# Merged strided loads of stacked operands, and earlier loads, in a two-layer encoder kernel

## The chip, the cores and the metric

The kernel runs on one core of one Trainium2 chip. The metric is the device time of one execution in microseconds (us). Three runs of the kernel before gave a median of 2371.69 us (2371.62 to 2374.82).

## What is computed

Two layers of a bidirectional encoder work on a sequence of 512 tokens, 1024 channels wide, in float32. Each layer is a half-step feed-forward network, a mixer with three kinds of attention, and a second half-step feed-forward network, every one between two RMS norms:

```python
for l in range(DEPTH):
    y = swiglu(rmsnorm(h, ffn1_pre_g[l]), ffn1_w_gu[l], ffn1_w_down[l])
    h = h + 0.5 * rmsnorm(y, ffn1_post_g[l])
    u = rmsnorm(h, mix_pre_g[l])
    proj = u @ w_in[l]
    qa, ka, va, qb, kb, vb, qc, kc, vc, gl = jnp.split(proj, split_at, axis=-1)
    oa = neighbourhood_attention(qa, ka, va, na_rpb[l])     # A: 8 heads of 64, with a bias table
    ob = sliding_window_attention(rope(qb), rope(kb), vb, sw_sink[l])    # B: 8 heads, 2 of k and v
    oc = differential_attention(rope(qc), rope(kc), vc, lam, ...)  # C: 4 heads, two softmax maps each
    gates = sigmoid(gl + b_gate[l])
    merged = sum over the branches of gate * (branch @ w_branch[l])
    h = h + rmsnorm(merged @ w_out[l], mix_post_g[l])
    y = swiglu(rmsnorm(h, ffn2_pre_g[l]), ffn2_w_gu[l], ffn2_w_down[l])
    h = h + 0.5 * rmsnorm(y, ffn2_post_g[l])
```

## The kernel before

**Precision.** Matmuls run on float32r operands. Each float32 operand is split in a high part (ScalarE copies it) and a low part (VectorE subtracts), and a product is two or three matmuls of such parts. For attention scores, where a head is only 64 channels deep, the two parts are stacked on the 128 partitions: a stack holds 64 rows of the high part above 64 rows of the low part. For keys there is a second stack with low above high. The score of a block is then two matmuls, with the query's stack against both stacks of the key (`softmax_pv`, L1675).

**Stages.** A layer passes through three pools of on-chip buffers: the feed-forward network ("f"), the projection ("p", `project`) and the mixer ("m", `mixer`). `project` computes u @ w_in for all blocks of 128 channels that the attention needs (QA, KA, VA, QB, KB, VB, QC, KC, VC, four or one of each), and keeps most of the results in DRAM: the high and low parts of a block as two tensors of 128 x 512 ("part", L1427), and the blocks of QC and KC as they are ("raw", L1474), since their rotary turn is done later. All these stores go through `store` (L1403) on GpSimd's DMA queue.

**The mixer's order.** `ORDER` is a list written out by hand of the units of work: `qa`, `qb` and `qc` load what one attention pair or head needs, `aa`, `ab` and `ac` are the attention itself, `ga`, `gb`, `gc` the gates, `ya`, `yb`, `yc` the products with w_branch. `do` traces one unit. A planner then orders each engine's instructions from this trace and its own estimate of times; that order is fixed in the program, on the engines and on the DMA queues alike. An engine that waits holds up everything behind it.

**The loads.** All loads of the mixer but those of weights go through SyncE's queue (SP). `restacked` (L1774) loads a stack in two halves of 64 partitions, one from the high tensor and one from the low (L1783, L1784): 30 stacks a layer, into 14 buffers "st". `rope` (L1762) loads a raw block (L1760), and a second time with the two halves of each map exchanged, in four loads of 32 partitions (L1768); it then multiplies by the cosine and sine tables (L1769, L1770) and adds (L1771). These blocks live in five buffers "tx". The tables are loaded at unit `kb` (`tables_in`, L1943). `ask` (L1729) loads the raw relative-position values of a head of A, at the unit `qa` of its own pair and behind its stacks; its DRAM side is a hand-made pattern of 8 x 16 rows of 2 KB. `biases` (L1732) builds from it an edge tile and a middle tile for the head, in buffers "g".

**What stands behind what.** In `softmax_pv`, VectorE makes the low part (L353) of the transposed weights, which TensorE multiplies at L1710. The weights of the dense products are split by L224 (ScalarE) and L225 (VectorE) and multiplied at L326 to L328.

Of the kernel before, what the change touches and what calls it, by code (L numbers as in the profile page):

```python
# [10 lines left out]
F32 = mybir.dt.float32  # L11
# [5 lines left out]
P = 128  # L17
# [3 lines left out]
T = 512  # L21
# [18 lines left out]
QA, KA, VA, QB, KB, VB, QC, KC, VC, GL = 0, 4, 8, 12, 16, 17, 18, 22, 26, 30  # L40
# [79 lines left out]
def encoder_kernel(ctx: ExitStack, tc: tile.TileContext, order, xT, wts, cols, rows, rpb, consts, tables, out):  # L120
    nc = tc.nc
# [5 lines left out]
    dr = ctx.enter_context(tc.tile_pool(name="dr", bufs=1, space=bass.MemoryType.DRAM))  # L127
# [19 lines left out]
    def nm(s):  # L147
        serial[0] += 1
        return f"{s}{serial[0]}"

    def big(tag, dt=F32, shape=(P, T), name="v"):
        if tag in BUFS:
            return sb.tile(list(shape), dt, tag=tag, name=nm(name), bufs=BUFS[tag])
        kind, pool = phase[0]
        return pool.tile(list(shape), dt, tag=tag, name=nm(name), bufs=ABUFS[kind][tag])
# [7 lines left out]
    V, A, G, PE = nc.vector, nc.scalar, nc.gpsimd, nc.tensor  # L163

    def f(t):
        return t.bitcast(F32)
# [94 lines left out]
    for l in range(L):  # L261
        for which in (1, 2):
            name = f"ffn{which}_w_down"
# [1104 lines left out]
    def project(l, op, accs):  # L1368
# [34 lines left out]
        def store(kind, x):  # L1403
            d = dr.tile([P, T], F32, tag=kind, name=nm(kind), bufs=60)
            G.dma_start(d, f(x))
            return d

        def parts(x):
            hi, lo = big("t", F32R, name="hi"), big("t", F32R, name="lo")
            A.activation(hi, x, AF.Copy)  # L1410
            V.tensor_tensor(out=lo, in0=x, in1=f(hi), op=ALU.subtract)
            return hi, lo

        def stacked(c, x):
            hi, lo = parts(x)
            if c in (QA, KA):
                made[c] = []
                for s in range(2):
                    own, res = slice(64 * s, 64 * s + 64), []
                    for one, two in ((hi, lo), (lo, hi))[: 1 if c == QA else 2]:  # L1420
                        st = slots.pop(0)
                        nc.sync.dma_start(f(st)[0:64], f(one)[own])
                        nc.sync.dma_start(f(st)[64:128], f(two)[own])
                        res.append(st)
                    made[c].append((res + [None])[:2])
                return
            made[c] = store("part", hi), store("part", lo)  # L1427

        def turned(c, x, heads):
            tp = bank("at")  # L1430
# [13 lines left out]
        turning, slowly, values = [], [], []  # L1444
# [19 lines left out]
        def ready(c, x):  # L1464
            if c >= GL:
                gated(c, x)
            elif c < VA:
                stacked(c, x)
            elif QB <= c < VB:
                turned_by(c, x)  # L1470
            elif c < KB or c >= VB and (c < QC or c >= VC):
                values.append(lambda: turned(c, x, 1 if c >= VC else 2))
            else:
                made[c] = store("raw", x)  # L1474

        def now():
            while values:
# [8 lines left out]
        made = {}  # L1486
# [38 lines left out]
        for n, c0 in (("cosR", 0), ("sinR", 512)):  # L1525
            t = big("rr", name=n)
# [108 lines left out]
        work(len(slowly))  # L1635
        return made

    def raw_of(l, hd):
        return bass.AP(rpb.tensor, (l * 8 + hd) * 16 * RPBW, [[RPBW, 8], [1, 16], [1, 8 * RPBW]])

# [76 lines left out]
    def mixer(l, op, made):  # L1717
# [3 lines left out]
        for n in range(3):  # L1721
            masks[n] = pre[:, n // 2, 256 * (n % 2) : 256 * (n % 2) + 256]

        def ask(hd):
            if hd < 2:
                raws[hd] = pre[:, 2 + hd, :]
                return
            raw = raws[hd] = big("g", name="braw")
            nc.sync.dma_start(raw, raw_of(l, hd))  # L1729

        def biases(hd):
            raw = raws.pop(hd)  # L1732
            if hd < 2:
                edge = made["edges"][:, hd, :]
                mid = made["edges"][:, 2, 2 * P * hd : 2 * P * (hd + 1)]
            else:
                edge = big("g", name="bedge")
                mid = big("g", shape=(P, 2 * P), name="bmid")

            def put(dst, mask, n0, n1):  # L1740

                src = raw[:, 7 * RPBW + 39 - 8 * n0 :]
                (ps0, pn), _ = src.ap
                V.tensor_tensor(
                    out=dst.rearrange("p (d r c) -> p d r c", r=8, c=8),
                    in0=bass.AP(src.tensor, src.offset, [[ps0, pn], [-8, n1 - n0], [-RPBW, 8], [-1, 8]]),
                    in1=mask.rearrange("p (d r c) -> p d r c", r=8, c=8),
                    op=ALU.add,
                )

            put(edge[:, 0:256], masks[0], 0, 4)
            put(mid, masks[1], 0, 4)
            put(edge[:, 256:384], masks[2][:, :P], 2, 4)
            put(edge[:, 384:512], masks[2][:, P:], 0, 2)
            return lambda i: edge[:, 0:256] if i == 0 else edge[:, 256:512] if i == NT - 1 else mid


        def load(d, dt=F32, tag="tx"):
            x = big(tag, dt, name="x")
            nc.sync.dma_start(f(x), d)  # L1760
            return x

        def rope(c):
            x = load(made[c])
            sh = big("tx", name="sh")
            for q in range(4):
                o = q ^ 1
                nc.sync.dma_start(sh[32 * q : 32 * q + 32], made[c][32 * o : 32 * o + 32])  # L1768
            V.tensor_tensor(out=x, in0=x, in1=turning[0], op=ALU.mult)  # L1769
            V.tensor_tensor(out=sh, in0=sh, in1=turning[1], op=ALU.mult)  # L1770
            V.tensor_tensor(out=x, in0=x, in1=sh, op=ALU.add)  # L1771
            return x

        def restacked(c, both):  # L1774
            if c in (QA, KA):
                return made[c]
            hi, lo = made[c]
            res = []
            for s in range(2):
                own, pair_ = slice(64 * s, 64 * s + 64), []  # L1780
                for one, two in ((hi, lo), (lo, hi))[: 2 if both else 1]:
                    st = big("st", F32R, name="st")
                    nc.sync.dma_start(f(st)[0:64], one[own])  # L1783
                    nc.sync.dma_start(f(st)[64:128], two[own])  # L1784
                    pair_.append(st)
                res.append((pair_ + [None])[:2])
            return res

        def values(c):
            t = made[c] if c == VA else [load(d, F32R, "st") for d in made[c]]  # L1790
            if c >= VC:
                return t
            v = [x.rearrange("p (b h d) -> p b h d", b=2, h=2) for x in t]
            return lambda j, s: v[j // 2][:, j % 2, s, :]
# [4 lines left out]
        def settle():  # L1799
            while pending:  # L1800
                pending.pop(0)()
# [4 lines left out]


        def qkv_a(p):
            got = restacked(QA + p, False), restacked(KA + p, True), values(VA + p)
            for s in range(2):  # L1810
                ask(2 * p + s)
            return got

        oa = [sb.tile([P, 4, T], F32R, tag="X", name=nm("oa"), bufs=BUFS["X"]) for _ in range(2)]

# [121 lines left out]
        def qkv_b(c):  # L1937
            return restacked(c, c == KB)

        def tables_in():  # L1940
            for n, c0 in (("cosR", 0), ("sinR", 512)):
                t = big("rr", name=n)
                nc.sync.dma_start(t, tables[:, c0 : c0 + T])  # L1943
                turning.append(t)
# [22 lines left out]
        def do(u):  # L1967
            kind, i = u[:2], int(u[2:] or 0)
            if kind == "fc" or kind[0] == "y":
                if kind == "fc" and i >= len(oc) or kind[0] == "y" and (kind[1], 3) not in OT:  # L1970
                    settle()
            if kind == "qa":
                held[u] = qkv_a(i)
            elif kind == "kb":
                tables_in()
                held["kb"] = qkv_b(KB), values(VB)
            elif kind == "qb":
                held[u] = qkv_b(QB + i)
            elif kind == "qc":
                held[u] = qkv_c(i)  # L1980
            elif kind == "aa":
                attn_a(i, *held.pop(f"qa{i}"))
            elif kind == "ab":
                attn_b(i, held.pop(f"qb{i}"), *held["kb"])
            elif kind == "ac":
                attn_c(*held.pop(f"qc{i}"))
            elif kind == "fc":
                finish_c(i)
            elif kind[0] == "g":
                gates("abc".index(kind[1]), i)  # L1990
            elif kind[0] == "y":
                combine("abc".index(kind[1]), kind[1], i)
# [15 lines left out]
        at = len(order) // HB  # L2008
# [56 lines left out]
        first = begin(H.X.blocks, firsts_of(l, 2), ("mm", "mx"), ((1, second_block), (KD - 2, last_block)))  # L2065
# [5 lines left out]
    for l in range(L):  # L2071
        with open_phase("f"):
            X, accs = ffn(l, 1, X, accs)
        with open_phase("p"):
            made = project(l, X, accs)
# [63 lines left out]
```

## Time and profile before

| | |
|---|---|
| median of three runs | 2371.69 us (2371.62 to 2374.82) |
| the profiled execution | 2370.88 us |
| its span, first to last instruction | 2369.1 us |
| mean granted TensorE clock | 0.996 |
| TensorE / VectorE / ScalarE / GpSimd busy | 99% / 80% / 61% / 9% |
| DMA | 395.16 MB, mean 167 GB/s |

The profile comes from one execution under the hardware profiler. PE is TensorE's matmuls, PEld its weight loads, DVE VectorE, ACT ScalarE, POOL GpSimd, SP SyncE; a "q" behind the name is the engine's sequencer, which waits and issues DMAs. `L1769` is a line of the kernel. `x<-raw` means that an instruction writes tile x and reads tensor raw. In lists of waits the columns are the total, the number and the longest, in us; in a timeline the start, the duration and in brackets the idle time before, with what ended it. A table of stretches gives the start and end, the length, the busy time of PE, PEld, DVE, ACT and POOL with instructions in brackets, the granted clock of TensorE as a share, the mean busy share of the 16 DMA engines (over 1 where packets overlap) and GB/s. A row of one line's instructions gives the shortest, median and longest duration in ns and the first and last start in us. DMA queue q1 is that of SP, q10 that of ScalarE, q0 that of GpSimd; a row of a queue gives packets, MB and busy share of the 16 engines, a row of issues the count, the size and the median us from issue to landing.

### The profile page before, as it was taken

To read this page: it belongs to the slowest core of one execution; us is meant where nothing else is said; L and a number is where in the kernel's file an instruction comes from. 1 tells how busy PE (TensorE), PEld (TensorE's weight loads), DVE (VectorE), ACT (ScalarE), POOL (GpSimd) and SP (SyncE) were. 2 spreads that over 40 slices of the span, in tenths; PEclk is the share of its full clock that TensorE was granted. 3 is DMA by queue.
4 is the path that set the end of the run, shared out by engine and by line. 5 is a ranking of instruction groups with operands and counts; after the bars stand their busy time and mean duration, and the time that the engine had idled before them with its cause. 6 is when DMAs were issued, how large, how long until landed. Compare 5 with 4: busy or idle time off the path is not lost. (4 is left out here: it accounts for less than half of the span.)

```text
span 2369.1 us, 40269 instructions
## 1 busy us (share of the span) xinstructions
PE 2342.6 (99%) x15134; PEld 2109.5 (89%) x15134; DVE 1892.4 (80%) x3082; ACT 1446.8 (61%) x2715; POOL 223.8 (9%) x354
## 2 busy tenths in 40 slices
PE   9999999999999999999999999999999999999998
PEld 8999889997888889998899998889978788899987
DVE  7887988966888668888878878889579876788796
ACT  6555566667777465655655554666687764556563
POOL 0111001110121001110001110011101200011100
PEclk9999999999999999999999999999999999999999
DMA  5566446667565524664525565276774664256642
GB/s 170 162 169 190 154 145 187 207 219 207 168 174 189 167 97 147 166 162 165 175 87 168 162 178 196 102 216 199 222 206 139 195 206 140 97 147 172 190 148 84
DMA packets 138147, 395.16 MB, mean 167 GB/s; under 512 B 19296, under 2 KB 26080, under 8 KB 137440
## 3 DMA queue, kind: packets, MB, share of 16 engines
q1 hardware_dynamic: 102960, 260.37, 35.0%
q0 software_dynamic: 20160, 78.66, 12.4%
q10 hardware_dynamic: 14832, 53.56, 7.4%
q8 instruction: 119, 1.95, 0.3%
q14 instruction: 76, 0.62, 0.1%
HBM read 326.98 MB, written 80.74 MB: 172 GB/s over the span
## 5 line engine op out<-in xcount | busy, mean ns | idle before, releaser
L680 PE MATMUL mm<-X,h 128*128 128x256 f32 x1504 | 268.0, 278 | 1.2 <-DVE v L738 1.2
L680 PEld LDWEIGHTS mm<-X,h 128*128 128x128 f32 x1504 | 228.5, 188 | 2.5 <-DVE v L738 2.0
L225 DVE TENSOR_TENSOR w<-wr,w 128x512 fp32r<-128x512 f32 x264 | 178.9, 685 | 56.2 <-ACT w L224 55.2
L224 ACT ACTIVATE w<-wr 128x512 fp32r<-128x512 f32 x264 | 162.5, 627 | 96.4 <-PE mm L328 40.8
L326 PE MATMUL mm<-X,w 128*128 128x512 f32 (+1 forms) x570 | 218.3, 383 | 1.8 <-ACT X L553 1.8
L328 PE MATMUL mm<-X,w 128*128 128x512 f32 (+1 forms) x570 | 216.4, 380 | 0.8 <-DVE w L225 0.8
L327 PE MATMUL mm<-X,w 128*128 128x512 f32 (+1 forms) x570 | 216.2, 379 | 0.8 <-DVE X L554 0.7
L680 PE MATMUL mm<-ht,h 128*128 128x256 f32 x752 | 210.1, 279 | 0.0
L680 PE MATMUL mm<-ht,l 128*128 128x256 f32 x752 | 210.1, 279 | 0.0
L680 PE MATMUL mm<-lt,h 128*128 128x256 f32 x752 | 209.4, 278 | 0.0
L680 PE MATMUL mx<-ht,h 128*128 128x256 f32 x752 | 208.3, 277 | 0.6 <-ACT v L724 0.6
L680 PE MATMUL mm<-X,l 128*128 128x256 f32 x752 | 208.2, 277 | 0.0
L680 PE MATMUL mx<-ht,l 128*128 128x256 f32 x752 | 208.1, 277 | 0.0
L680 PE MATMUL mx<-lt,h 128*128 128x256 f32 x752 | 207.9, 277 | 0.0
L630 DVE TENSOR_TENSOR l<-wr,h 128x1024 fp32r<-128x1024 f32 x94 | 114.9, 1222 | 65.7 <-PE mm L680 65.7
L662 ACT ACTIVATE h<-wr 128x1024 fp32r<-128x1024 f32 x94 | 99.9, 1062 | 78.7 <-PE mx L680 55.5
L680 PE MATMUL at<-X,w 128*128 128x256 f32 x1128 | 144.2, 277 | 0.0
L680 PEld LDWEIGHTS mx<-ht,h 128*128 128x128 f32 x752 | 141.2, 188 | 1.4 <-ACT v L724 1.4
L680 PEld LDWEIGHTS mm<-ht,l 128*128 128x128 f32 x752 | 141.7, 188 | 0.1
L680 PEld LDWEIGHTS mm<-ht,h 128*128 128x128 f32 x752 | 141.7, 188 | 0.0
L680 PEld LDWEIGHTS mm<-lt,h 128*128 128x128 f32 x752 | 141.7, 188 | 0.0
L680 PEld LDWEIGHTS mx<-ht,l 128*128 128x128 f32 x752 | 141.2, 188 | 0.2 <-DVE l L640 0.2
(458 smaller groups left out, 6802.4 us busy)
## 6 DMA issues: line engine op xcount, KB each, us to landing
wr<-in_wts_dram SPq DMA_DIRECT2D x273, 512.0 KB, 4.6
wr<-in_wts_dram ACTq DMA_DIRECT2D x102, 512.0 KB, 4.1
sum<-in_wts_dram POOLq DMA_DIRECT2D x64, 512.0 KB, 5.3
st<-part SPq DMA_DIRECT2D x120, 128.0 KB, 5.1
ap<-in_wts_dram SPq DMA_DIRECT2D x20, 512.0 KB, 5.6
a<-kept SPq DMA_DIRECT2D x32, 256.0 KB, 6.3
ap<-sum SPq DMA_DIRECT2D x16, 512.0 KB, 4.3
x<-part SPq DMA_DIRECT2D x32, 256.0 KB, 3.8
```

The source lines that it names most:

```text
L224: A.activation(hi, raw, AF.Copy)
L225: V.tensor_tensor(out=lo, in0=raw, in1=f(hi), op=ALU.subtract)
L326: PE.matmul(acc, w[0], x[0], start=start, stop=False)
L327: PE.matmul(acc, w[0], x[1], start=False, stop=False)
L328: PE.matmul(acc, w[1], x[0], start=False, stop=stop)
L630: V.tensor_tensor(out=w["l1"], in0=self.raws[g][0], in1=f(w["h1"]), op=ALU.subtract)
L662: A.activation(self.W[g]["h24"], self.raws[g][1], AF.Copy)
L680: PE.matmul(acc, ws[i], xs[j], start=start and k == m == 0, stop=stop and k == n - 1 and m == 2, skip_group_check=True,)
```

## The change

Four things change, all between the projection and the mixer's attention:

- **Stacks by one strided transfer.** The parts of a block are stored in one DRAM tensor, high rows, then low rows, and for keys the high rows a third time. A stack is then one load of 128 partitions, whose DRAM side is a pattern made by `halves`: two runs of 64 rows, 128 rows apart.
- **Raw blocks twice.** A QC or KC block is stored twice, in rows interleaved so that the block and the block with exchanged halves are each one load by `halves`, at row 0 and at row 32.
- **Biases a pair ahead.** The raw values of heads 2 and 3 are asked for with the first pair, ahead of the stacks, and so on; the middle tiles of two heads share one buffer.
- **Tables and first raw blocks.** The rotary tables and the two loads each of the first QC and the first KC block are issued at unit `qa1` instead of at `kb` and `qc0`.

```diff
@@ project: stacked, ready
-            made[c] = store("part", hi), store("part", lo)
+            n = 2 + (KA <= c < VA or c == KB)
+            d = dr.tile([n * P, T], F32, tag=f"both{n}", name=nm("both"), bufs=60)
+            for at, t in enumerate((hi, lo, hi)[:n]):
+                G.dma_start(d[P * at : P * at + P], f(t))
+            made[c] = d
...
-                made[c] = store("raw", x)
+                made[c] = dr.tile([2 * P, T], F32, tag="raw", name=nm("raw"), bufs=60)
+                for n in range(2):
+                    G.dma_start(halves(made[c], 64 * n), f(x))
...
+    def halves(d, row):
+        pitch = d.ap[0][0]
+        return bass.AP(d.tensor, d.offset + row * pitch, [[P * pitch, 2], [pitch, 64], [1, T]])
@@ mixer: biases, rope, restacked, qkv_a, do
+        mids = []
...
-                mid = big("g", shape=(P, 2 * P), name="bmid")
+                if hd % 2 == 0:
+                    mids.append(big("g", name="bmid"))
+                mid = mids[-1][:, 2 * P * (hd % 2) : 2 * P * (hd % 2) + 2 * P]
...
+        def begun(c):
+            x = load(halves(made[c], 0))
+            sh = big("tx", name="sh")
+            nc.sync.dma_start(sh, halves(made[c], 32))
+            return x, sh
+
+        first = {}
+
         def rope(c):
-            x = load(made[c])
-            sh = big("tx", name="sh")
-            for q in range(4):
-                o = q ^ 1
-                nc.sync.dma_start(sh[32 * q : 32 * q + 32], made[c][32 * o : 32 * o + 32])
+            x, sh = first.pop(c, None) or begun(c)
...
-            hi, lo = made[c]
             res = []
             for s in range(2):
-                own, pair_ = slice(64 * s, 64 * s + 64), []
-                for one, two in ((hi, lo), (lo, hi))[: 2 if both else 1]:
+                pair_ = []
+                for n in range(2 if both else 1):
                     st = big("st", F32R, name="st")
-                    nc.sync.dma_start(f(st)[0:64], one[own])
-                    nc.sync.dma_start(f(st)[64:128], two[own])
+                    nc.sync.dma_start(f(st), halves(made[c], P * n + 64 * s))
                     pair_.append(st)
...
         def qkv_a(p):
-            got = restacked(QA + p, False), restacked(KA + p, True), values(VA + p)
-            for s in range(2):
-                ask(2 * p + s)
-            return got
+            for hd in ((0, 1, 2, 3), (4, 5), (6, 7), ())[p]:
+                ask(hd)
+            return restacked(QA + p, False), restacked(KA + p, True), values(VA + p)
...
             if kind == "qa":
+                if i == 1:
+                    tables_in()
+                    first.update((c, begun(c)) for c in (QC, KC))
                 held[u] = qkv_a(i)
             elif kind == "kb":
-                tables_in()
                 held["kb"] = qkv_b(KB), values(VB)
```

## The prediction

> **What bounds the kernel now.** I read the page first, then the busy time by stage, the waits of PE, the timelines around the longest wait, and the DMA view of that stage.
>
> ```profile
> span 2369.1 us, 40269 instructions
> PE 2342.6 (99%) x15134; PEld 2109.5 (89%) x15134; DVE 1892.4 (80%) x3082; ACT 1446.8 (61%) x2715; POOL 223.8 (9%) x354
> ```
>
> PE is busy 2342.6 of 2369.1 us. Nothing that shortens a load can win more than the 26.5 us in which PE is idle. The profiled execution took 2370.88 us, 1.8 us around its span and 0.03% under the median of 2371.69; the sum below is made against 2371.
>
> The change touches the mixer. These are its attention stretches in layers 0 and 1 (columns: PE, PEld, DVE, ACT, POOL busy, granted clock, DMA share, GB/s):
>
> ```profile
> 514.00:720.00 206.00, 201.53 (x1070) 169.16 (x1068) 160.78 (x457) 153.31 (x389) 30.01 (x56) 0.98 0.67 190
> 1690.00:1900.00 210.00, 204.75 (x1078) 171.04 (x1077) 164.93 (x465) 156.32 (x393) 30.59 (x58) 0.99 0.67 184
> ```
>
> About 5 us idle in each, and a clock a little below full. The waits of PE name one place, and the timelines of PE and DVE show it in both layers:
>
> ```profile
> PE o L1710 <- DVE lo L353: 6.9, 2, 3.7
> ...
> PE o L1892 <- DVE lo L353: 1.2, 1, 1.2
> ...
> 557.87 0.58 PE L1710 MATMUL o<-lo,x 128*128 128x256 f32 x1 [3.67 <-DVE lo L353]
> ...
> 556.73 0.69 DVE L1769 TENSOR_TENSOR x<-x,cosR 128x512 f32<-128x512 f32 x1 [5.60 <-DMA x<-raw]
> 557.34 0.17 DVE L1692 RECIPROCAL l<-l 128x4 f32<-128x4 f32 x1
> 557.43 0.39 DVE L353 TENSOR_TENSOR lo<-at,hi 128x256 fp32r<-128x256 f32 x1
> ...
> 1729.85 0.39 PE L1710 MATMUL o<-lo,x 128*128 128x256 f32 x1 [3.21 <-DVE lo L353]
> ...
> 1728.70 0.69 DVE L1769 TENSOR_TENSOR x<-x,cosR 128x512 f32<-128x512 f32 x1 [5.13 <-DMA x<-raw]
> ```
>
> DVE stands 5.60 us at the first rotary multiply, whose block has not landed, and the low half that PE needs is queued behind it. The clock is then halved for a while:
>
> ```profile
> 556.50:563.33 6.83, 5.46 (x14) 4.45 (x15) 3.00 (x9) 3.34 (x8) 0.00 (x0) 0.50 0.93 218
> 1730.69:1734.10 3.41, 3.41 (x9) 2.67 (x9) 1.58 (x5) 2.17 (x6) 0.00 (x0) 0.50 0.98 217
> ```
>
> **Part 1: tables, first raw blocks and biases earlier.** The tables and the four loads of the first two rotary blocks move from behind the third pair's stacks to ahead of the second pair's. If they land, 3.67 + 3.21 us of waiting go, and half of 6.83 + 3.41 us at half clock: 6.9 + 5.1 = **12.0 us**. Next late in the mixer is, by the same view, the 1.2 us at L1892. The shared middle bias tile saves buffers and no instruction; the rpb loads go a pair earlier. Both cost nothing on PE, since no row of PE waits for a bias. But on SP's queue everything moved now stands ahead of the second pair's stacks, which part 3 needs.
>
> **Part 2: more stores.** Each layer gets four third copies (KA+1 to KA+3, KB) and eight second raw stores, 24 more on POOL in all:
>
> ```profile
> L1405 POOL DMA_DIRECT2D raw<-v x8: 542/542/542, 459.2 to 1673.6; - x8
> ...
> L1729 SPq DMA_DIRECT2D braw<-in_rpb_dram x12: 622/643/665, 526.5 to 1733.4; - x12
> ...
> L1784 SPq DMA_DIRECT2D st<-part x60: 444/594/1198, 495.8 to 1770.0; - x60
> ```
>
> 24 x 0.54 = 13 us of POOL, which is busy 9%, and nobody waits soon for these stores: nothing. SP issues 60 stack loads where it issued 120, and 16 rotated loads where it issued 64. Even if one strided issue costs what a bias load costs (643 ns, also a hand-made pattern), SP gains; it sets no end, so nothing.
>
> **Part 3: the shape of the merged loads.** This decides. A merged load reads DRAM as 2 runs of 64 rows: its outermost dimension is 2. Before, all loads have 32, 64 or 128 rows outermost, but one: the bias load reads 8 x 16 rows. The DMA view of 514 to 720 us lets one count what an outermost 8 does:
>
> ```profile
> DMA packets 16984, 39.13 MB, mean 190 GB/s; under 512 B 3118, under 2 KB 3118, under 8 KB 16965
> ...
> q1 hardware_dynamic: 10592, 17.83, 32.1%
> ...
> st<-part SPq DMA_DIRECT2D x58, 128.0 KB, 4.9
> x<-part SPq DMA_DIRECT2D x14, 256.0 KB, 4.6
> ...
> x<-raw SPq DMA_DIRECT2D x8, 256.0 KB, 3.6
> sh<-raw SPq DMA_DIRECT2D x32, 64.0 KB, 2.0
> ...
> braw<-in_rpb_dram SPq DMA_DIRECT2D x6, 256.0 KB
> ...
> cosR<-in_tables_dram SPq DMA_DIRECT2D x1, 256.0 KB, 7.4
> sinR<-in_tables_dram SPq DMA_DIRECT2D x1, 256.0 KB
> x<-gate SPq DMA_DIRECT2D x1, 256.0 KB
> ```
>
> Every row here is 2 KB, so SP's 121 loads are 58 x 64 + 14 x 128 + 8 x 128 + 32 x 32 + 6 x 128 + 3 x 128 = 8704 row packets. Queue q1 has 10592; 1888 are left, tiny ones. If each load ended with one on each of 16 engines there would be 121 x 16 = 1936. The 48 missing are 6 x 8: 115 loads ended on 16 engines and the six bias loads on 8. So the outermost dimension caps the engines, and I read the merged loads as running on **2 engines of 16**, 64 rows (131 KB) each.
>
> By the Trainium skill, "DMA: Bandwidth & Descriptors", section "Why a DMA increments its semaphore by 16 and not by 1", a DMA runs on the largest number up to 16 that divides the slowest dimension of both patterns, and from SP on the lowest-numbered engines. The count above agrees with the first half at 8; no run here shows 2. That rule speaks against the change, and by it the sum is the one that follows.
>
> Which two? No view numbers the engines. The first x<-raw was issued behind two bias loads:
>
> ```profile
> 544.95 1.81 SPq L1729 DMA_DIRECT2D braw<-in_rpb_dram  x2
> ...
> 548.06 0.43 SPq L1760 DMA_DIRECT2D x<-raw  x1
> ```
>
> It landed by 556.73, some 8.7 us after issue, where the median of its kind is 3.6. If bias loads took their engines in turn, two of them would have spread like one weight load. I take it that it is always the same engines, and so that all merged loads share one pair.
>
> The rate of one engine comes from three rows: the whole engine set in its fullest microsecond of this stage, in one of its fullest stretches anywhere, and q1 in the stack stretch, 516 to 640 us:
>
> ```profile
> 553.00:554.00 1.00, 1.00 (x6) 0.59 (x4) 0.00 (x0) 0.30 (x2) 0.00 (x0) 1.00 1.04 361
> ...
> 766.00:768.00 2.00, 2.00 (x16) 1.83 (x16) 1.97 (x4) 1.09 (x3) 0.00 (x0) 1.00 1.04 417
> ...
> DMA packets 11170, 24.25 MB, mean 196 GB/s; under 512 B 1886, under 2 KB 1886, under 8 KB 11159
> ...
> q1 hardware_dynamic: 8179, 13.88, 42.1%
> ...
> x<-raw SPq DMA_DIRECT2D x3, 256.0 KB, 3.6
> sh<-raw SPq DMA_DIRECT2D x12, 64.0 KB, 2.3
> ```
>
> 361 / (16 x 1.04) = 21.7 GB/s, so 6.0 us a load; 417 / 16 = 26.1, so 5.0 us; 13.88 MB / (0.421 x 16 x 124 us) = 16.6, so 7.9 us under full contention. I take 6.0: while the stage is stretched, the other traffic thins out, but it does not go.
>
> When are the loads wanted?
>
> ```profile
> 516.27 0.44 SPq L1783 DMA_DIRECT2D st<-part  x1
> ...
> L1675 PE MATMUL mx<-st,st x112: 274/282/442, 531.2 to 646.8; 128*128 128x256 f32 x80, 128*128 128x384 f32 x32
> ...
> L1769 DVE TENSOR_TENSOR x<-x,cosR x8: 675/681/692, 556.7 to 718.8; 128x512 f32<-128x512 f32 x8
> ```
>
> - *516 to 640 us*, before the last head of the stacks: 30 stack loads (60 of L1784 in two layers) and the four early raw loads, 34 x 6.0 = 204 us on each of the two engines. Their share of the rest: 24.25 MB less the 9.2 MB of stack, raw and rotated loads in that stretch (58 x 128 KB, 3 x 256 KB, 12 x 64 KB), over 16, is 0.94 MB, 43 us. 247 us of work for 124: **123 us late**. Fourteen stack buffers let SP run ahead by under two pairs, so the lateness cannot be hidden by starting sooner; and the first score matmul on stacks, 15 us after the loads begin, waits at once.
> - *640 to 720 us*, the rotary blocks of heads 1 to 3: 12 loads, 72 us. The rest: 39.13 - 24.25 = 14.9 MB less 2.6 of raw and rotated loads, over 16, 0.77 MB, 36 us. 108 us for 80: **28 us late**.
>
> PE's order is fixed, and no work of PE stands behind to fill in, so lateness is PE idle. 151 us a layer, 302 in two, less the 12.0 of part 1: 2371 + 302 - 12 = **2661 us**. At 5.0 us a load: (170 + 36 - 124) + (60 + 29 - 80) = 91 a layer, 2541. At 7.9: (269 + 57 - 124) + (95 + 46 - 80) = 263 a layer, 2885. The half clock after each wait adds nothing while the loads are what is late; where they are not, it takes the time up.
>
> **The rivals.**
> - *Sixteen engines after all* (the pattern is cut up again before it reaches the engines, so part 3 does not happen): 2371 - 12 = 2359 us, faster. For it: the stall is real and the loads for it now start some 30 us sooner. The Trainium skill's same page, "Rules for kernel authors", says that two transfers to halves of the partitions should rather be one over 128, which is this outcome; no row here shows such a pair merged. Against it: the six bias loads were not cut up again. The point that decides is the wire time of a merged load: under 124 / (34 + 43 / 6.0) = 3.0 us nothing is late in the stack stretch, and over it lateness there grows by some 41 us a layer for each us. Chance 0.09.
> - *Two engines, taken in turn*: no engine is overfull, each load only lands some 3 us later (5.0 to 7.9 us of wire where 4.9 was the median landing). Stacks are asked for 15 us or more ahead and stand it; the rotary chain of heads 1 to 3, four loads a head, may give 12 us a head and all of the gain back: from 2359 to 2359 + 72, about 2385. Against it: the 8.7 us above. Chance 0.07.
> - *The wait only moves*: the early loads land, but stand ahead of the second pair's stacks on SP, and PE waits there for what it saved: 2371. For it: 15 us between 516.27 and 531.2. Chance 0.04.
>
> **How the numbers follow.** The overfull pair of engines has 0.80 and is the forecast, 2661. Its own range is 2541 to 2885; the unknown clock and a start of some loads before 516 us widen it, and a part of the in-turn case lies near its foot: 2490 to 2940 should hold the time 8 times in 10. About 0.2% is what a measurement of this kernel can tell from no change. Slower: 0.80 and most of the in-turn case, 0.86. Faster: nearly all of the sixteen-engine case, 0.09. Same: 0.05, from the moved wait.
>
> **What the changed profile would show.** Right: q1's tiny packets fall to 2 for each merged load; st and x landings in tens of us; PE waiting for st loads in the mixer for 100 us or more a layer, the granted clock often 0.50 there, the other stages unchanged. Part 1 right: no 5.6 us wait at L1769's first multiply. Wrong: st loads landing in 5 us with DMA share near 0.67, or a mixer of some 206 us.

## The result, and the profile after

| | before | after |
|---|---|---|
| median of five runs | 2371.62 us (2366.04 to 2374.82) | 2757.03 us (2754.78 to 2762.81) |
| ratio, 95% interval | | 1.1638 (1.1614 to 1.1662) |
| the profiled execution, its span | 2370.88, 2369.1 us | 2762.81, 2761.0 us |
| mean granted clock | 0.996 | 0.931 |

The kernel became 385 us slower. The forecast was 2661 us, with a range of 2490 to 2940 and a chance of 0.86 for slower: side and range held, and 96 us more were lost than forecast.

The page after begins with these two lines:

```profile
span 2761.0 us, 40158 instructions
PE 2412.5 (87%) x15134; PEld 2159.3 (78%) x15134; DVE 1901.4 (69%) x3082; ACT 1447.3 (52%) x2715; POOL 244.3 (9%) x378
```

TensorE runs the same 15134 matmuls. It is idle for 348.5 us of the span (2761.0 - 2412.5), where it was 26.5, and busy for 69.9 us more (2412.5 - 2342.6), because the clock fell in the stretches with waits. 322 + 70 is the whole difference of 392 us in the span.

The waits of PE, which named one place of 6.9 us before, now begin like this:

```profile
PE mx L1685 <- DMA st<-both: 154.1, 19, 19.8
PE o L1720 <- DVE lo L353: 53.9, 7, 14.0
PE o L1907 <- DVE lo L353: 35.7, 6, 11.5
PE o L1906 <- ACT hi L352: 29.0, 4, 7.5
PE mx L680 <- ACT v L724: 28.7, 4, 7.7
```

L1685 is the score matmul on the stacks (L1675 before): 19 waits of up to 19.8 us for merged loads. L1720, L1906 and L1907 belong to the weighted sums of the attention. Their longest waits come from the merged raw loads: VectorE stands at a rotary multiply whose block has not landed, and what PE needs is made behind it. So the 11.5 and the 14.0 us are of the same kind as the 3.7 us of before, only longer; the part on why the prediction was right shows one of them. The last line belongs to the projection, where the forecast had put nothing.

The stretch of 514 to 720 us after, by engine (columns as in the tables of stretches), and the same stretch's transfers:

```profile
514.00:720.00 206.00, 98.87 (x502) 85.32 (x502) 58.39 (x173) 62.99 (x170) 7.60 (x12) 0.70 0.30 99
```

```profile
GB/s 206 200 165 131 193 143 213 190 74 120 126 50 137 51 73 114 50 156 101 50 50 50 50 50 121 67 52 49 50 49 95 93 49 52 50 136 49 49 53 220
```

PE is busy for 98.87 us where it was 201.53. The second fence is the traffic in 40 slices. In 18 of them it stands at 49 to 53 GB/s. SP's timeline shows what paces it:

```profile
546.52 0.52 SPq L1774 DMA_DIRECT2D x<-raw  x1
547.21 0.51 SPq L1780 DMA_DIRECT2D sh<-raw  x1
547.82 6.48 SPq L1774 DMA_DIRECT2D x<-raw  x1
...
559.43 7.51 SPq L1741 DMA_DIRECT2D braw<-in_rpb_dram  x2
567.03 30.77 SPq L1800 DMA_DIRECT2D st<-both  x6
597.91 5.65 SPq L1774 DMA_DIRECT2D x<-part  x2
```

The first two merged loads of the stretch take 0.52 and 0.51 us to issue, the third 6.48. So the pattern isn't slow to issue in itself: SP is held once merged loads are under way ahead. Six merged loads then take SP 30.77 us to issue, 5.1 us each; before, one half load mostly took 0.4 to 0.6 us. 262144 bytes in 5.1 us are 51 GB/s, which is the floor of the traffic above. The two value loads behind them (L1774) take 5.65 us where such a pair took 0.99 us before.

The packets of SP's queue, counted over the whole execution, before and after, tell on how many engines the merged loads ran:

```profile
q1 hardware_dynamic: 102960, 260.37, 35.0%
```

```profile
q1 hardware_dynamic: 99944, 260.36, 28.8%
```

The bytes and the 2 KB rows are the same, so the difference of 3016 is in the tiny packets that end each load on each of its engines. Gone are 120 half stacks, 16 plain raw blocks and 64 rotated quarters, on 16 engines each: 200 x 16 = 3200. Come are 60 + 16 + 16 = 92 merged loads. 3200 - 3016 = 184 = 92 x 2. Every merged load ended on two engines.

Where the time was lost is read from the first and last start of the same matmuls. In layer 0 these are, before, the scores on the "early" stacks (which need no merged load) and the scores of C (L1865, L1866); and after, the early scores, the scores on stacks and those of C:

```profile
L1675 PE MATMUL mx<-early x8: 274/283/384, 516.6 to 522.3; 128*128 128x256 f32 x8
...
L1865 PE MATMUL mx<-st,st x32: 387/393/501, 649.5 to 756.6; 128*128 128x512 f32 x32
```

```profile
L1685 PE MATMUL mx<-early x8: 280/283/384, 546.8 to 552.6; 128*128 128x256 f32 x8
...
L1685 PE MATMUL mx<-st,st x112: 274/338/582, 596.3 to 797.6; 128*128 128x256 f32 x80, 128*128 128x384 f32 x32
...
L1880 PE MATMUL mx<-st,st x32: 388/393/628, 810.2 to 952.9; 128*128 128x512 f32 x32
```

- Up to the first early score, all of it before the attention: 546.8 - 516.6 = 30 us.
- Up to the last score on stacks: 797.6 - 646.8 = 151 us, so 121 us in the stack stretch.
- Up to the last score of C: 952.9 - 756.6 = 196 us, so 45 us in the rotary stretch.

Layer 1, taken from a matmul ahead of its projection (L544, at 1505.4 us before and 1704.8 after), gives 23, 122 and 45 us by the same rows.

### The profile page after: what moved, and what is told of

Same layout as the page of the kernel before. It is cut to its first block, busy times and chain, and to the rows that moved or that the text cites. A ratio compares the mean times of both kernels' runs of the same rounds, so it can differ in the third digit from the quotient of the medians.

```text
span 2761.0 us, 40158 instructions
## 1 busy us (share of the span) xinstructions
PE 2412.5 (87%) x15134; PEld 2159.3 (78%) x15134; DVE 1901.4 (69%) x3082; ACT 1447.3 (52%) x2715; POOL 244.3 (9%) x378
## 3 DMA queue, kind: packets, MB, share of 16 engines
q0 software_dynamic: 36416, 85.07, 12.1%
## 4 chain that ended last, share of the span: by engine, by line
PE 55%; issue 17%; DMA 11%; DVE 3%; ACT 1%; POOL 1%; SPq 0%; DVEq 0%; POOLq 0%; ACTq 0%
PE mm L680 13%; PE mx L680 6%; DMA sh<-raw 6%; PE mm L1152 5%; DMA wr<-in_wts_dram 4%; PE mm L326 4%; PE mm L327 4%; PE mm L328 4%; PE mx L1152 3%; PE at L680 3%; PE at L1152 3%; PE at L327 2%; PE at L326 2%; PE at L328 2%; PE o L1152 1%
## 5 line engine op out<-in xcount | busy, mean ns | idle before, releaser
L326 PE MATMUL mm<-X,w 128*128 128x512 f32 (+1 forms) x570 | 226.1, 397 | 2.6 <-ACT X L553 1.7
L327 PE MATMUL mm<-X,w 128*128 128x512 f32 (+1 forms) x570 | 224.8, 394 | 0.8 <-DVE X L554 0.7
L328 PE MATMUL mm<-X,w 128*128 128x512 f32 (+1 forms) x570 | 223.6, 392 | 0.0
L1685 PE MATMUL mx<-st,st 128*128 128x256 f32 (+1 forms) x224 | 60.4, 361 | 163.6 <-DMA st<-both 154.1
L1685 PEld LDWEIGHTS mx<-st,st 128*128 128x128 f32 x224 | 43.4, 223 | 174.4 <-DMA st<-both 88.6
L352 ACT ACTIVATE hi<-at 128x256 fp32r<-128x256 f32 (+2 forms) x160 | 70.1, 443 | 185.3 <-PE o L1719 92.0
L621 DVE TENSOR_TENSOR r<-wr,wr 128x1024 f32<-128x1024 f32 x94 | 115.1, 1224 | 45.4 <-DMA wr<-in_wts_dram 39.1
```

What stands on the lines that cost most here:

```text
L326: PE.matmul(acc, w[0], x[0], start=start, stop=False)
L327: PE.matmul(acc, w[0], x[1], start=False, stop=False)
L328: PE.matmul(acc, w[1], x[0], start=False, stop=stop)
L352: A.activation(hi, src, AF.Copy)
L621: V.tensor_tensor(out=w["r13"], in0=base, in1=r[0], op=ALU.add)
L1685: PE.matmul(shaped(sp, k), qs, k, start=m == 0, stop=m == 1)
```

## The experiments

**The parts alone.** Four kernels ran beside the kernel before: three with one part of the change each, and one with the whole change but without its merged transfers.

*Stacks only:* the kernel before with merged stack loads and third copies.

```diff
...
-                for one, two in ((hi, lo), (lo, hi))[: 2 if both else 1]:
+                for n in range(2 if both else 1):
                     st = big("st", F32R, name="st")
-                    nc.sync.dma_start(f(st)[0:64], one[own])
-                    nc.sync.dma_start(f(st)[64:128], two[own])
+                    nc.sync.dma_start(f(st), halves(made[c], P * n + 64 * s))
...
```

> Only the stacks are loaded by one strided transfer (with the three-part stores they need); raw blocks, tables and biases as before. Theory E: the stack stretch is late by some 100 to 120 us a layer as in the changed kernel, with four strided loads fewer in it, and the rotary stretch is not: 2371 + 200 to 240 = 2571 to 2611 us; the 5 us wait for the first raw block stays or hides in it. Theory O: 2371 us, nothing has moved. Theory S: eight of the 24 stores, a third of the slowdown, 2500 us.

Measured: 2579.33 against 2368.65 us, ratio 1.0886 (1.0866 to 1.0905). The merged stacks alone cost 211 us.

*Raw blocks only:* the kernel before with raw blocks stored twice and loaded whole.

```diff
-                made[c] = store("raw", x)
+                made[c] = dr.tile([2 * P, T], F32, tag="raw", name=nm("raw"), bufs=60)
+                for n in range(2):
+                    G.dma_start(halves(made[c], 64 * n), f(x))
...
-            x = load(made[c])
+            x = load(halves(made[c], 0))
...
-            for q in range(4):
-                o = q ^ 1
-                nc.sync.dma_start(sh[32 * q : 32 * q + 32], made[c][32 * o : 32 * o + 32])
+            nc.sync.dma_start(sh, halves(made[c], 32))
```

> Only the raw blocks are stored twice by strided stores and loaded by strided loads; stacks, tables and biases as before. Theory E: the projection is late by 23 to 29 us a layer (strided stores hold the buffers that ScalarE writes next) and the rotary stretch by some 45, so 2371 + 2 x 71 = 2513 us (2480 to 2550). Theory O: 2371 us. Theory S: 16 of the 24 stores, two thirds of the slowdown, 2630 us.

Measured: 2509.41 against 2368.65 us, ratio 1.0593 (1.0571 to 1.0615), 141 us.

*The order only:* the kernel before, with its own shapes, but with the biases a pair ahead and the tables and first raw blocks at the unit `qa1`.

```diff
...
+            for hd in ((0, 1, 2, 3), (4, 5), (6, 7), ())[p]:
+                ask(hd)
-            got = restacked(QA + p, False), restacked(KA + p, True), values(VA + p)
-            for s in range(2):
-                ask(2 * p + s)
-            return got
+            return restacked(QA + p, False), restacked(KA + p, True), values(VA + p)
...
             if kind == "qa":
+                if i == 1:
+                    tables_in()
+                    first.update((c, begun(c)) for c in (QC, KC))
                 held[u] = qkv_a(i)
             elif kind == "kb":
-                tables_in()
```

> Only the order changes: tables and first raw blocks with the second pair, biases a pair ahead, one middle tile for two heads; all loads keep the shape of before. Theory E: the first rotary wait goes, 2359 us (2353 to 2366). Theory O: most of the slowdown is here, over 2600 us. Theory S: 2359 us.

Measured: 2378.49 against 2368.65 us, ratio 1.0038 (1.0025 to 1.0051). It was expected to win 12 us and loses 10.

*All but the merging:* the whole change, with each strided load and store made as two of 64 rows.

```diff
...
-                    nc.sync.dma_start(f(st), halves(made[c], P * n + 64 * s))
+                    for h in range(2):
+                        row = P * (n + h) + 64 * s
+                        nc.sync.dma_start(f(st)[64 * h : 64 * h + 64], made[c][row : row + 64])
...
```

> Everything of the change stays, but each strided load and each strided store goes as two of 64 rows. Theory E (few engines: outermost dimension 2 puts a load on two DMA engines): the whole slowdown goes and the 12 us of the first rotary wait are won, 2359 us (2350 to 2368). Theory O (order: tables and first raw blocks stand ahead of the second pair's stacks): the stacks are as late as in the changed kernel, over 2700 us. Theory S (24 more stores): over 2700 us as well, since they are all still there.

Measured: 2383.78 against 2368.65 us, ratio 1.0061 (1.0046 to 1.0076). All the large loss is in the merged transfers, loads and stores, and the gain of the new order doesn't appear without them either. The parts alone add up: 211 + 141 + 10 = 362 of the 385 us.

**Why the merged loads are slow: the shape or the queue.** *Rows first* is the stacks-only kernel with the two outer dimensions of the pattern exchanged. It is still one load of 128 rows for each stack, but now with 64 outermost; a stack's high and low rows alternate on the partitions, in queries and keys alike.

```diff
-        return bass.AP(d.tensor, d.offset + row * pitch, [[P * pitch, 2], [pitch, 64], [1, T]])
+        return bass.AP(d.tensor, d.offset + row * pitch, [[pitch, 64], [P * pitch, 2], [1, T]])
```

> The twin of the stacks-only kernel (2579 us): the same three-part stores and one strided load a stack, but the pattern has its two dimensions exchanged, 64 rows outermost and the two parts inside, so a stack's rows alternate high and low (queries and keys alike; a score sums over them). Theory E: 64 rows outermost spread over 16 engines, so nothing is late: 2369 us (2360 to 2376), with some 5 us landings. Theory M (merging itself is bad, one load of 256 KB is slower to land or to issue than two of 128 KB): 2579 us, as its twin.

Measured: 2375.04 against 2369.56 us, ratio 1.0022 (1.0013 to 1.0031). One line takes the loss from 211 us to 5. SP's packets over the whole execution, of stacks only and then of rows first:

```profile
q1 hardware_dynamic: 101160, 260.36, 31.5%
```

```profile
q1 hardware_dynamic: 102000, 260.37, 34.8%
```

and the issues of their stack loads, in the same order:

```profile
L1790 SPq DMA_DIRECT2D st<-both x60: 482/5099/8855, 493.6 to 1963.9; - x60
```

```profile
L1790 SPq DMA_DIRECT2D st<-both x60: 512/556/1633, 494.8 to 1760.5; - x60
...
DMA to landing us min/median/max: 2.9/7.0/8.6
```

With the half loads gone (120 x 16 = 1920 tiny packets of 102960), stacks only has 120 in their place, 2 a load; rows first has 960, 16 a load. With 16 engines the issue takes 556 ns, with two 5099. So the outermost dimension of the pattern decides, not the strides, the size or the number of loads.

*The other queue* is the stacks-only kernel with its merged loads issued on GpSimd's queue: `G.dma_start(f(st), ...)` for `nc.sync.dma_start(f(st), ...)`.

> The stacks-only kernel (2579 us) with the same strided loads, two runs outermost, issued from GpSimd's queue instead of SP's. The prediction took it that a load of this shape always gets the same two engines. If that holds for any queue, 2579 us (2550 to 2620). If GpSimd's queue takes its two engines in turn, no pair is overfull and the loads only land later: 2375 to 2420 us.

Measured: 2409.35 against 2366.62 us, ratio 1.0178 (1.0161 to 1.0195). The same pattern costs 43 us there, not 211. For 514 to 720 us the view of transfers has

```profile
st<-both POOLq DMA_DIRECT2D x30, 256.0 KB, 11.9
```

No load is held for long: the median lands 11.9 us after issue, and of 40 slices of the traffic one stands near 50 GB/s (53), where it was 18 in the changed kernel. Two engines taken in turn would do that. The Trainium skill, "DMA: Bandwidth & Descriptors", section "Why a DMA increments its semaphore by 16 and not by 1", states such a rule: always the lowest-numbered engines on SP's queue, and on GpSimd's a cursor that goes round. The times agree with both halves. But GpSimd's queue also makes the transfer differently, as its packets over the whole execution show, of stacks only and then of this kernel:

```profile
q0 software_dynamic: 20800, 80.76, 11.7%
```

```profile
q0 software_dynamic: 52480, 96.71, 15.5%
```

(52480 - 20800) / 60 = 528 packets a load, where SP's queue used 128 and 2. From these the engines of one load can't be counted. That the loads take two engines in turn there, and not more engines at once, is argued, not shown.

**What the stores cost.** *Raw stores only* is the raw-only kernel with its loads made as pairs of 64 rows, so that only the strided stores on GpSimd's queue are left of the merging.

```diff
-            x = load(halves(made[c], 0))
-            sh = big("tx", name="sh")
-            nc.sync.dma_start(sh, halves(made[c], 32))
+            x, sh = big("tx", name="x"), big("tx", name="sh")
+            for t, row in ((x, 0), (sh, 32)):
+                for h in range(2):
+                    nc.sync.dma_start(t[64 * h : 64 * h + 64], made[c][row + P * h : row + P * h + 64])
```

> Of the raw-only kernel (2509 us) only the strided stores stay; each block is loaded by loads of 64 rows. If the strided stores on GpSimd's queue are what makes the projection late, 23 to 29 us a layer stay: 2369 + 52 = 2421 us (2405 to 2430), with ScalarE waiting for buffers at L724 and the rotary stretch as before. If the projection is late for something else, 2369 us.

Measured: 2411.03 against 2369.56 us, ratio 1.0171 (1.0157 to 1.0185). The stores cost 41 us, and the merged raw loads the other 98 (2509 - 2411). The place is the projection. First the wait of PE there in this kernel (0.6 us in all before), then the landing of SP's weight loads from 440 to 515 us, before and in this kernel:

```profile
PE mx L680 <- ACT v L724: 30.1, 4, 9.2
```

```profile
L211 SPq DMA_DIRECT2D wr<-in_wts_dram x12: 327/328/527, 444.2 to 494.8; - x12
...
DMA to landing us min/median/max: 3.5/3.8/4.5
```

```profile
L211 SPq DMA_DIRECT2D wr<-in_wts_dram x12: 327/328/527, 446.1 to 511.2; - x12
...
DMA to landing us min/median/max: 4.5/7.6/11.4
```

The weights land 4 us later in the median. ScalarE splits them, in order, and the copy that PE waits for stands behind. From 440 to 560 us ScalarE waits 20.0 us for these weights at L650 (6.6 before), and for no store, so it is not the stores' own buffers that hold it. In the changed kernel its timeline shows the step, and PE's the wait that follows:

```profile
476.51 0.63 ACT L650 ACTIVATE w<-wr 128x512 fp32r<-128x512 f32 x1 [7.49 <-DMA wr<-in_wts_dram]
477.05 1.04 ACT L625 ACTIVATE h<-wr 128x1024 fp32r<-128x1024 f32 x1
478.00 0.36 ACT L724 ACTIVATE v<-mx 128x256 f32<-128x256 f32 x1
```

```profile
478.41 0.58 PE L680 MATMUL mx<-ht,h 128*128 128x256 f32 x1 [6.35 <-ACT v L724]
```

**Where the 12 us of part 1 went.** The order-only kernel does remove the wait it was made for: L1710's goes from 6.9 to 0.6 us in all (below). Its SP timeline around the start of the attention:

```profile
515.32 7.28 SPq L1772 DMA_DIRECT2D sh<-raw  x4
522.71 0.37 SPq L1764 DMA_DIRECT2D x<-raw  x1
523.18 1.76 SPq L1772 DMA_DIRECT2D sh<-raw  x4
525.05 1.33 SPq L1731 DMA_DIRECT2D braw<-in_rpb_dram  x2
526.47 0.51 SPq L1793 DMA_DIRECT2D st<-part  x1
```

and the waits and the scores on stacks that follow:

```profile
PE o L1709 <- ACT hi L352: 6.5, 5, 2.0
PE mx L1675 <- issue: 4.5, 1, 4.5
...
PE mx L1675 <- DMA st<-part: 2.7, 2, 2.4
...
PE o L1710 <- DVE lo L353: 0.6, 2, 0.3
```

```profile
L1675 PE MATMUL mx<-st,st x224: 274/283/562, 539.8 to 1822.8; 128*128 128x256 f32 x80, 128*128 128x384 f32 x32
```

The rotated block occupies SP for 7.28 us, and the second pair's stacks go out from 526.47 where they went out from 516.27. The first score on stacks comes at 539.8, not 531.2. At L1675 PE now waits 7.2 us (for 4.5 of them the profile names no cause), where 6.3 were saved at L1710, and at L1709 6.5 us. The wait has moved ahead. Five more kernels took part 1 apart:

*Biases only:* the biases a pair ahead and the shared middle tile, nothing else.

> Of the order-only kernel (2378 us) only the biases a pair ahead and the shared middle tile. If the early tables and raw blocks are what costs there (they hold SP ahead of the second pair's stacks), this one costs nothing, and it gains if the first raw block then no longer stands behind two bias loads: it should land some 3 us sooner, so 2369 - 2 x 3 and some clock, 2361 us (2357 to 2369). If the biases are what costs, 2378 us.

*Early blocks only:* tables and first raw blocks at `qa1`, ahead of the second pair's stacks, the biases as before.

> Of the order-only kernel (2378 us) only the early tables and raw blocks. If they hold SP ahead of the stacks: 2375 us (2370 to 2382), the first score on stacks some 9 us late. If the biases are what costs there: 2357 us, the wait at the first rotary multiply gone.

*Early behind the stacks:* the same, behind the second pair's stacks.

```diff
             if kind == "qa":
+                held[u] = qkv_a(i)
                 if i == 1:
                     tables_in()
                     first.update((c, begun(c)) for c in (QC, KC))
-                held[u] = qkv_a(i)
```

> Of the change only the early tables and first raw blocks, all loads in the shape of before, and issued at the same unit but behind the second pair's stacks instead of ahead of them. Theory H (SP's order: what stands ahead of the stacks makes them late): the stacks come as before, the first rotary wait goes, 2369 - 12 = 2357 us (2354 to 2364). Theory N (in the mixer every wait of a few us that goes comes back elsewhere, as in the biases-only kernel, 2375 us): 2369 to 2376 us.

*Rows first, early behind the stacks of pair 2:* the same edit on the rows-first kernel.

> The stacks by one load with 64 rows outermost (2375 us alone) and the early tables and raw blocks behind the second pair's stacks. Theory H: 2375 - 12 = 2363 us or better, since SP has half the stack loads to issue. Theory N: 2372 to 2380 us.

*Rows first, early behind the stacks of pair 3:* with `if i == 2`.

> As the kernel with rows outermost and early loads behind the stacks, but the early loads one unit later, behind the third pair's stacks. Theory H: 2363 us as well, or a little less, since the second and the third pair's stacks are both ahead. Theory N: 2372 to 2380 us.

| kernel | median, us | before, us | ratio, 95% interval |
|---|---|---|---|
| biases only | 2374.65 | 2369.56 | 1.0021 (1.0011 to 1.0030) |
| early blocks only | 2382.57 | 2369.56 | 1.0056 (1.0042 to 1.0070) |
| early behind the stacks | 2376.53 | 2366.37 | 1.0039 (1.0026 to 1.0051) |
| rows first, early behind pair 2's | 2374.29 | 2366.37 | 1.0036 (1.0023 to 1.0049) |
| rows first, early behind pair 3's | 2373.10 | 2366.37 | 1.0026 (1.0014 to 1.0038) |

None wins. The kernel with biases only shortens L1710's wait too, and pays with a new one, as its waits of PE show:

```profile
PE mx L1675 <- DMA st<-part: 4.8, 2, 3.3
...
PE o L1710 <- DVE lo L353: 1.3, 3, 0.6
```

Its second pair's stacks go out from 519.23 us, 3 us later than before. In both kernels a transfer that is issued earlier on SP makes the stacks behind it late, and about what was saved at L1710 is paid at L1675. Why each of these variants ends 0.2 to 0.6% above the kernel before, instead of level with it, these runs do not settle. One candidate is the order of the engines' instructions, which the planner makes anew for each of them. No version here is faster than the kernel before.

## Why the prediction was right in the main, and where it was wrong

- **Two engines, always the same (part 3): right.** The packet counts give 2 engines for each of the 92 merged loads, and 16 as soon as 64 stands outermost. The engines also had to be the same ones for the loads to pile up, and two rows show that: the third merged load is held for 6.48 us when two are under way (engines taken in turn would have been free for it), and the floor of 50 GB/s, at 5.1 us a load, is what a pair that works alone leaves. The 8.7 us of the first raw load, on which the forecast put the choice between the same two and two in turn, pointed the right way. The rival of sixteen engines fell with the count.
- **The stack stretch: 123 us a layer forecast, 121 and 122 measured, but partly by luck.** A load takes 5.1 us, not the 6.0 taken. With the bytes of the other traffic at the same rate (43 x 5.1 / 6.0 = 37 us) the forecast's own sum gives 34 x 5.1 + 37 - 124 = 86 us. The other 35 us the sum did not have. In both layers 35 us are lost before the first score on stacks: in layer 0 it comes 49.5 us after the first early score (596.3 - 546.8), where it came after 14.6 (531.2 - 516.6). Two waits there give 30 of them: 14.0 us at the early rotary blocks (part 1 below), and 15.7 for the first stacks, which SP issues behind those blocks. But this isn't the price of the early blocks alone. Stacks only, which moves none, has its first score on stacks after 16.1 us (531.4 - 515.3), and still takes 226.5 us from the first early score to the last on stacks, where it was 130.2. That is 96 us more, where the sum for 30 loads gives 66 (30 x 5.1 + 37 - 124). SP stands still in the issue of each merged load, so biases and value loads behind it go out late too. How much of the excess that is, no run measures by itself.
- **The rotary stretch: 28 us a layer forecast, 45 measured.** The raw loads by themselves cost 98 us in two layers, as the pair of raw kernels shows, so the mechanism is the forecast's and its size was too small; with 5.1 us a load its sum gives only 12 (12 x 5.1 + 31 - 80). The sum compared the pair's work with the length of the stretch. The runs show a chain instead: VectorE waits for a block, then for its rotated copy, 55.5 us at L1787 and 78.6 at L1788 over the whole execution, and PE waits behind it.
- **Part 2, "nobody waits soon for these stores: nothing": this step failed.** Nobody waits for the stores, but the stores delay others. The raw stores alone cost 41 us, and in the changed kernel the projection is 30 and 23 us late. The step counted 24 more issues at 0.54 us each and asked who waits for their data. It did not ask what a strided store is on that queue, nor which loads run beside it: the weights that the projection is reading. What it is in the stores that slows these loads, the runs do not show.
- **Part 1, minus 12.0 us: this step failed too.** The wait at L1710 can be removed, as the runs on the order show, but what is moved ahead on SP holds back the second pair's stacks. That is the rival "the wait only moves", which had 0.04. The forecast had named these stacks as standing behind everything that moves, and still charged nothing. In the changed kernel itself the early blocks are not in time either: their rotary multiplies, and the wait of PE behind them, are

```profile
557.73 0.69 DVE L1787 TENSOR_TENSOR x<-x,cosR 128x512 f32<-128x512 f32 x1 [2.19 <-DMA x<-raw]
...
562.99 0.69 DVE L1788 TENSOR_TENSOR sh<-sh,sinR 128x512 f32<-128x512 f32 x1 [4.17 <-DMA gate<-gate]
569.38 0.69 DVE L1787 TENSOR_TENSOR x<-x,cosR 128x512 f32<-128x512 f32 x1 [5.70 <-DMA x<-raw]
...
574.83 0.69 DVE L1788 TENSOR_TENSOR sh<-sh,sinR 128x512 f32<-128x512 f32 x1 [4.16 <-DMA sh<-raw]
575.44 0.42 DVE L353 TENSOR_TENSOR lo<-at,hi 128x256 fp32r<-128x256 f32 x1
...
575.91 0.58 PE L1720 MATMUL o<-lo,early 128*128 128x256 f32 x1 [14.01 <-DVE lo L353]
```

  The 5.60 us ahead of the first have become 2.19, but three more waits follow, and the low part that PE needs stands behind all four. So the wait that part 1 was to remove, PE's for a low part behind the first rotary multiplies, grew from 3.67 to 14.01 us, and in layer 1 from 3.21 to 13.93. Of the 4.17 ahead of the second multiply the profile names a gate's transfer as the last to come. The 12.0 itself was also 0.7 too high: 1.4 us of the 3.67 lie in the stretch at half clock and were counted there again by half.
- **"The half clock after each wait adds nothing while the loads are what is late": wrong over the whole execution.** The same matmuls took 70 us more of PE's time. A part of that stands where PE would else have been idle, waiting for loads; how much of it came on top, these runs do not separate.
- **The sum.** Forecast 2 x (123 + 28) - 12 = 290 us. (Its faster bound used 26.1 GB/s without the share of 1.04 by which the first rate was divided; with it the bound is 25.1 GB/s, 5.2 us a load.) Measured by the starts of the matmuls: 30 + 121 + 45 in layer 0 and 23 + 122 + 45 in layer 1, 386 us of the 392 in the span. The difference of 96 is the projection (53), the rotary stretch (34) and part 1's gain that did not come (12), less 3 in the stack stretch.
- **The signs.** Two tiny packets a merged load and the low clock came as forecast. PE's waits for stacks are 154.1 us in two layers, so 77 a layer and not 100: the rest of its idle time stands at the steps behind. That the other stages would be unchanged was wrong. The landing of the merged loads can't be read, since the view of transfers gives none for loads on two engines.

## What to carry to other kernels

Before two transfers are merged into one, look at the outermost dimension of the pattern: on SP's queue it caps the engines, and the pattern of 2 x 64 rows ran at 51 GB/s and cost 211 us, and the same rows as 64 x 2 ran on sixteen engines and cost 5. The rule of the Trainium skill, "DMA: Bandwidth & Descriptors", "Rules for kernel authors", that two transfers to halves of the partitions should be one over 128, needs the row for using all 16 engines in the same table, which asks for a multiple of 16 outermost: with it the merged stacks cost 1.0022 times the time before, without it 1.0886. For a store, ask not only who waits for it, but whose loads run beside it; and for a load that is moved ahead on a full queue, charge what it passes.

## What the runs showed of the hardware that was not expected

- **SP's issue is held when merged loads are under way on two engines.** The first two issued in 0.52 and 0.51 us, but the median issue took 5136 ns in the changed kernel, as long as the load itself, against 556 ns with the stack loads on sixteen engines (rows first), and everything behind it on the queue waits:

```profile
L1800 SPq DMA_DIRECT2D st<-both x60: 493/5136/10285, 567.0 to 2104.5; - x60
```

- **A strided store on GpSimd's queue is many small packets.** The changed kernel has 36416 - 20800 = 15616 packets more on that queue than stacks only, with 32 strided stores in place of 16 plain ones of 80: (15616 + 16 x 80) / 32 = 528 a store, as many as a merged load has there. Of a load's 528, 464 are under 512 bytes (the pages count 45344 packets under 512 bytes in the kernel on the other queue and 17624 in stacks only; with the 120 of SP's that are gone, 27840 / 60). That a plain store of the same block on that queue has 80 comes from the third copies: stacks only has eight more stores than before, and 20800 - 20160 = 640 packets more. Its issue costs more as well, in the changed kernel against 542 ns before:

```profile
L1480 POOL DMA_DIRECT2D raw<-x x16: 828/837/847, 461.8 to 1892.5; - x16
...
DMA to landing us min/median/max: 8.7/13.7/17.5
```

- **One engine moved 25.5 GB/s when its pair worked alone** (51 GB/s over two), in the upper part of the 16.6 to 26.1 that the forecast had worked out from the stage before.
